# A hybrid decoder layer on one core: mix-out product by halves of its features, square and token sums at later places, and two seven-product feature pairs in each gate-value product with half of their weight sums added by DMA

## The chip, the core and the metric

The kernel runs on one core of a Trainium2 chip. The metric is the device time of one execution in microseconds (us), smaller is better. Before the change three runs gave 2009.51, 2010.1 and 2012.91 us, a median of 2010.1 us.

The engines are named as in the profile: PE (TensorE, matmuls; PEld is its weight load), DVE (VectorE), ACT (ScalarE), POOL (GpSimd) and SP (SyncE, which issues nearly all transfers). A queue name with a q (SPq) is the engine's sequencer.

## What is computed

One decoder layer for 256 tokens of width 2048, all in float32, with a batch of one and depth one:

```python
h = x
hn = rmsnorm(h, norm_mix_w)
q, k, v, g_ret, xr, yr, g_a, g_b = split(hn @ w_in)          # 2048 x 14336
ret = head_groupnorm(chunkwise_retention(rotary(q), rotary(k), v), ret_gn_w)
ret_out = silu(g_ret) * ret
hr = rg_lru(causal_dwconv(xr, rnn_conv_w, rnn_conv_b), ...)  # gated linear recurrence
rnn_out = gelu(yr) * hr
merged = sigmoid(g_a) * (ret_out @ w_proj_ret) + sigmoid(g_b) * (rnn_out @ w_proj_rnn)
h = h + merged @ w_mix_out
h = h + memory_cross_attention(rmsnorm(h, norm_xa_w), rmsnorm(mem, norm_mem_w), ...)
up = causal_dwconv(rmsnorm(h, norm_ffn_w) @ ffn_w_up, ...)   # 2048 x 11264: gate | value
gate, val = split(up)
h = h + (silu(gate) * val) @ ffn_w_down                      # 5632 x 2048
return rmsnorm(h, final_norm_w)
```

## The kernel before

**Precision.** Each float32 operand is split into a high part (a cast to fp32r) and a low part (the rest), and a product is three matmuls: high by high, low by high, high by low. Weights are split in `weight_parts` (lines 338 to 345): ACT casts `hi` (L343), DVE subtracts to get `lo` (L344). The parts stand in six buffers each, `PART_BUFS`.

**Weight stream.** All weights lie in one array in HBM, in the order in which they are used. `prefetch` (L267) takes them in chunks of 1 MB through SP's queue into one of three `raw` buffers, two chunks ahead of the product that uses them. A chunk of a plain product (`steps_n`) holds four feature tiles of 128 rows by 512 columns; a chunk of a paired product (`steps_pair`, L469) holds two feature tiles (a k-pair) of two column blocks. Such a chunk costs PE 24 matmuls of 128 x 512.

**Seven products.** In a paired product, a k-pair, two halves of the tokens and two column blocks make a product of 2 x 2 blocks by 2 x 2 blocks. For the k-pairs named in a tuple such as `SEVEN = (2, 5)` it is done with seven block products in place of eight, so 21 matmuls in place of 24. This needs sums of tokens (`sums_of`, L436: four DVE operations, one more on DVE and one on ACT for the split, and one DVE addition where only the split parts are at hand) and sums of weights (`seven_parts`, L358): from the blocks b12, b11, b22, b21 of the chunk DVE makes four sums in place (L364), b11+b12, b12+b22, b11+b12+b22 and b11+b12+b22+b21, each 128 x 512. A chunk in seven products has three and a half `hi`/`lo` pairs of 128 x 1024 to make, a plain one two. `token_sums` (L434) keeps every sum by its tile, so that a second product with the same tokens finds it. The queries, values and gates are made by paired and plain products, the eleven gate-value products of the FFN (`up`, L1229) by paired ones with `SEVEN_U = (4,)`.

**Buffers.** Most activations come out of one pool of 29 slots of 4 KB per partition, called `big`; smaller ones out of a pool of ten, `tmp`. A slot is free again when the last reader of its tile is done. PSUM has three double banks (`acc`) and two single banks (`small`); a paired product takes all three and both.

**Work beside the products.** `later(n, fn)` (L371) puts work n+1 chunks behind the current one. `by_dma` (L538) turns a [tokens, features] block into [features, tokens]: ACT writes 16-bit planes (`pl`, L546), two transposing DMAs on SP's queue write `pt`, and one or more chunks later `join` has ACT put the words together again (`f`, L559) and hands them on, to `turn_merged` (L969) for the merged gates.

**Order around the mix-out product.** The last product ahead of it is the second pair of `w_proj_ret` (L987), which gives the merged features of blocks 2 and 3. They reach PE through `by_dma` and `turn_merged`, block 2 joined behind one chunk (wait 1), block 3 behind three (wait 3). `residual` (L997) multiplies with `w_mix_out`, four column blocks of four chunks each. With `in_turn` (L125) the stream holds the first three chunks of blocks 0 and 1, then the last of each, then blocks 2 and 3. At the same place SP loads the residual rows (`hrow`, L993) and the memory rows (`mnat`, L994), and `memory_steps` (L1034) has ACT sum the squares of the memory rows (`sum_squares`, L632) in the first four chunks of the product.

**Recurrence.** In the loop at L911, `recur` (L877) makes for each feature tile two small matmul groups into a `small` bank, which ACT reads at once (`tr`, L889, and `ti`, L890; `ti` is a `big` tile).

Of the kernel before, what the change touches and what calls it, by code (L numbers as in the profile page):

```python
# [14 lines left out]
ALU = mybir.AluOpType  # L15
AX = mybir.AxisListType

P = 128
# [22 lines left out]
EARLY = [2, 2, 4, 4, 4]  # L41
SEVEN = (2, 5)
SEVEN_O = (3, 5)
SEVEN_U = (4,)

O_Q, O_K, O_V, O_G = 0, 1024, 2048, 4096
O_XR, O_YR, O_GA, O_GB = 6144, 8192, 10240, 12288
# [18 lines left out]
    return c  # L66


def both(w, c, seven=SEVEN, row=0, nk=NT, apart=BW):

    return w, row, nk, (c, c + apart, seven)


def weight_plan():

    plan = []
    for g in range(2):
        keys = [("w_in", 0, NT, c + g * BW) for c in (O_Q, O_K)]
        values = [("w_in", 0, NT, O_V + b * BW) for b in range(2)]
        plan += keys + [both("w_in", O_V + 1024)] if g else [keys[0], values[0], keys[1], values[1]]  # L80
        plan.append(both("w_in", O_G + g * 1024))
    for b in range(4):
        plan += [("w_in", 0, NT, c + b * BW) for c in (O_XR, O_YR)]
    plan += [("w_in", 0, NT, O_GB + b * BW) for b in range(2)] + [both("w_proj_rnn", 0)]
    plan += [both("w_in", O_GB + 1024), both("w_proj_rnn", 1024)]
    plan += [both(w, c + b * BW) for w, c in (("w_in", O_GA), ("w_proj_ret", 0)) for b in (0, 2)]
    plan += [("w_mix_out", 0, NT, b * BW) for b in range(4)]
    plan += [(w, 0, NT, b * BW) for b in range(4) for w in ("xa_w_k", "xa_w_q")]
    plan += [("xa_w_v", 0, NT, b * BW) for b in range(4)]
    plan += [both("xa_w_o", 0, SEVEN_O)] + [("xa_w_o", 0, NT, b * BW) for b in (2, 3)]  # L90
    for kind, *a in ff_plan():
        if kind == "down" and sum(a) < NF // 4:
            plan += [both("ffn_w_down", b * BW, SEVEN, a[0] * BW, 4 * a[1]) for b in (0, 2)]
        elif kind == "down":
            plan += [("ffn_w_down", a[0] * BW, 4 * a[1], b * BW) for b in range(4)]
        else:
            plan.append(both("ffn_w_up", a[0] * BW, SEVEN_U, apart=FF))
    return plan


# [26 lines left out]
    return [c for o in products for c in o[:-1]] + [o[-1] for o in products]  # L127


def weight_stream():  # L130

    out = [
        [(w, row + k * P, n, (*c[:2], k // KH in c[2]) if isinstance(c, tuple) else c) for k, n in pieces(i, nk, c)]
        for i, (w, row, nk, c) in enumerate(weight_plan())
    ]
    out[:2] = [[one for pair in zip(*out[:2]) for one in pair]]
    out[-4:-1] = [in_turn(out[-4:-1])]
    i = [c[0][0] for c in out].index("w_mix_out")
    out[i : i + 2] = [in_turn(out[i : i + 2])]
    return [one for chunks in out for one in chunks]  # L140


def chunk(inputs, name, row, n, c):

    if isinstance(c, tuple):
        a, b = (chunk(inputs, name, row, n, one) for one in c[:2])
        order = (b[:, 0], a[:, 0], b[:, 1], a[:, 1]) if c[2] else (a[:, 0], a[:, 1], b[:, 0], b[:, 1])
        return np.stack(order, axis=1)
# [11 lines left out]
def hybrid_layer(  # L160
# [106 lines left out]
    def prefetch(n):  # L267
        while len(ahead) < n and taken[0] < len(stream):
            i = taken[0]
            name, row, nk, c = stream[i]  # L270
            taken[0] += 1
            if i == 0:
                both = wp.tile([P, KC, BW], F32, tag="raw", bufs=RAW_BUFS, name=nm("raw"))
                flat = both.rearrange("p k n -> p (k n)")[:, 0 : NT + KH * (S + BW)]
                cut = NT + S + BW
                for cs in (slice(0, cut), slice(cut, NT + KH * (S + BW))):
                    load(flat[:, cs], head[:, cs], True)
                both = flat[:, NT:].rearrange("p (k n) -> p k n", k=KH)
                scale0.append(flat[:, 0:NT])
                landed.append(flat[:, 0:1])  # L280
                raw = both[:, :, S:]
                xs.raw.append(both[:, :, 0:S])
            else:
                if isinstance(c, tuple):
                    nk *= 2
                size = nk * P * BW
                src = wall[at[0] : at[0] + size].rearrange("(p k n) -> p k n", p=P, k=nk)
                at[0] += size
            if i == 0:
                pass  # L290
            elif i < 4:
                raw = big([P, KH, BW], s="raw")
                if i == 1:
                    landed.append(raw[:, 0, 0:1])
                elif i == 2:
                    behind_of(raw, landed[0])
                    tc.keep_in_program_order(pool.tensor_copy(pa[:, 0:NT], scale0[0]))
            else:
                raw = wp.tile([P, KC, BW], F32, tag="raw", bufs=RAW_BUFS, name=nm("raw"))
            k2 = row // (KH * P)  # L300
            early = i < 2 * len(EARLY)
            own = early and i % 2 == 0
            cuts = () if i == 0 else range(0, nk + 1, KH) if i < 6 else (0, nk)
            if own:
                xs.load(k2 + 1)
            for a, b in zip(cuts, cuts[1:]):
                with tc.issue_after(behind[-1]) if i in in_order else nullcontext():
                    load(raw[:, a:b, :], src[:, a:b, :], early)
                if own and a == 0:
                    xs.load(k2 + nk // KH)  # L310
            if i >= 6:
                load_x(min(4, 2 * i - 11))
            if i == 8:
                load(cid, consts[:, 0:C_DEC], True)
                load(pa[:, 16:P], by_feature[:, 16:P], True)
                load(pb, by_feature[:, P : P + 80], True)
            if i == 13:
                load(pf.rearrange("p a n -> p (a n)"), by_feature[:, P + 80 :], True)
            if i in (8, 9):
                for b in (2 * i - 16, 2 * i - 15):  # L320
                    sum_squares(xin[b], ss0, b)
            if isinstance(c, tuple) and c[2]:
                ahead.append(((row, c), seven_parts(raw)))
                continue
            parts = []
            for k in range(0, nk, KH):
# [31 lines left out]
    def seven_parts(raw):  # L358
# [7 lines left out]
        q2, q4 = weight_parts(raw[:, 2:4])  # L366
        return [p1, p3, p2, q1, q3, q2, q4]

    pending, step = [], [0]

    def later(n, fn):  # L371
# [3 lines left out]
    def chunks(nk, w, row, c):  # L375
# [4 lines left out]
        for k, n in pieces(i, nk, c):  # L380
            prefetch(1)
            (r_, c_), parts = ahead.pop(0)
            assert (r_, c_) == (row + k * P, (*c[:2], k // KH in c[2]) if isinstance(c, tuple) else c)
            prefetch(AHEAD)
            yield k, n, parts
            step[0] += 1
# [79 lines left out]
            sums_of(t, src, scale)  # L466
        out.append(t)

    def steps_pair(w, row, st, nk, c1, c2, seven=SEVEN):  # L469

        last = max(seven)
        banks, begun = {}, set()
# [8 lines left out]
                begun.add(name)  # L481

        o1 = o2 = None
        for k0, n, parts in chunks(nk, w, row, (c1, c2, seven)):
# [322 lines left out]
    for g in range(2):  # L807
# [16 lines left out]
                v = gemm_n("w_in", 0, xs, NT, O_V + b * BW) if b else ended(v_steps)  # L824
                vs.append(split_rows(v, rs0))
        if g == 1:
            vs += [split_rows(v, rs0) for v in pair("w_in", 0, xs, NT, O_V + 1024, O_V + 1024 + BW)]
        qr, kr = turned
        gates = []
        c = O_G + g * 1024  # L830
        for a in pair("w_in", 0, xs, NT, c, c + BW):
# [3 lines left out]
            dve.scalar_tensor_tensor(out=a, in0=t, scalar=1.0, in1=a, op0=ALU.add, op1=ALU.mult)  # L835
            gates.append(a)
        retain(g, qr, kr, vs, dec, gates)


    lam = pb[:, 0:16]  # L840
# [70 lines left out]
    for b in range(4):  # L911
# [28 lines left out]
        def gelu_y(f, xr=xr):  # L940
# [29 lines left out]
        for pr in range(2):  # L970
            merged.append(split_pair(f[:, 2 * pr : 2 * pr + 2, :], 0.5))

    ts = [tanh_rows(big([P, 2, BW], s="sig"), gemm_n("w_in", 0, xs, NT, O_GB + b * BW)) for b in range(2)]
    mb = []
# [22 lines left out]
    def residual(w, st, out, wcol, steps=None):  # L997
# [231 lines left out]
    def up(b, hid, seven):  # L1229
# [4 lines left out]
            conv(f, NF + 4 * b, vl)  # L1234
            gate_up(gt, vl, hid, seven)

        two = pair("ffn_w_up", 0, h2s, NT, b * BW, FF + b * BW, SEVEN_U)
# [62 lines left out]
```

## Time and profile before

| What | Value |
|---|---|
| Median of 3 runs | 2010.1 us (2009.51 to 2012.91) |
| Profiled execution, its own time | 2011.37 us |
| Its span in the profile | 2009.4 us |
| PE busy | 1971.7 us (98%), 8831 matmuls |
| DVE busy | 1564.5 us (78%) |
| ACT busy | 1370.1 us (68%) |
| POOL busy | 25.4 us (1%) |
| Read from HBM | 388.39 MB, 194 GB/s over the span |

The page gives busy time by engine, the span in forty slices, the chain of work that ended last, and the costliest groups of instructions. A group's line reads: source line, engine, operation, what it writes and reads, shape, count, then busy time, mean ns of one, and the idle time ahead of them with its releaser. A row of the view of waits reads: who waited, for whom, us in total, times, longest. A row of the timeline reads: start, length, engine, line, operation, tiles, count, and in brackets the idle time before it with its releaser. A row of the view of windows gives for each stretch its length, the busy time of each engine, the granted PE clock, the share of the DMA engines' time and GB/s. A row of transfers gives the count, the size of one and the median time from issue to landing.

### The profile page before, as it was taken

To read this page: it belongs to the slowest core of one execution; us is meant where nothing else is said; L and a number is where in the kernel's file an instruction comes from. 1 tells how busy PE (TensorE), PEld (TensorE's weight loads), DVE (VectorE), ACT (ScalarE), POOL (GpSimd) and SP (SyncE) were. 2 spreads that over 40 slices of the span, in tenths; PEclk is the share of its full clock that TensorE was granted. 3 is DMA by queue.
4 is the path that set the end of the run, shared out by engine and by line. 5 is a ranking of instruction groups with operands and counts; after the bars stand their busy time and mean duration, and the time that the engine had idled before them with its cause. 6 is when DMAs were issued, how large, how long until landed. Compare 5 with 4: busy or idle time off the path is not lost.

```text
span 2009.4 us, 24019 instructions
## 1 busy us (share of the span) xinstructions
PE 1971.7 (98%) x8831; PEld 1635.7 (81%) x8831; DVE 1564.5 (78%) x2044; ACT 1370.1 (68%) x1671; POOL 25.4 (1%) x25
## 2 busy tenths in 40 slices
PE   9999999998999999699999999999999999999998
PEld 8888788887888888588888888888888888888887
DVE  6887987898788888557546568678889868899686
ACT  6666658987645656568666666877877477874683
POOL 0000001000000000000000000000000000000000
PEclk9999999999999999899999999999999999999999
DMA  8756566666465465868666665756666656666673
GB/s 329 234 212 176 207 223 199 199 202 206 169 229 189 170 228 189 272 209 255 216 199 210 198 194 200 235 199 212 208 223 212 235 189 218 204 223 223 221 238 119
DMA packets 197190, 425.62 MB, mean 212 GB/s; under 512 B 142032, under 2 KB 146640, under 8 KB 152016
## 3 DMA queue, kind: packets, MB, share of 16 engines
q1 hardware_dynamic: 197072, 424.09, 63.2%
q8 instruction: 69, 1.13, 0.2%
q14 instruction: 49, 0.40, 0.1%
HBM read 388.39 MB, written 2.10 MB: 194 GB/s over the span
## 4 chain that ended last, share of the span: by engine, by line
PE 92%; DVE 3%; ACT 2%; issue 1%; DMA 1%; SPq 0%; POOL 0%; POOLq 0%; DVEq 0%; ACTq 0%
PE acc L245 67%; PE sm L245 25%; DVE lo L344 1%; ACT hi L343 1%; ACT f L559 0%; DMA nat<-in_mem 0%; ACT pl L546 0%; DVE tb L728 0%; DVE xr L925 0%; PE warm L242 0%; DVE rows L572 0%; DMA pt<-pl 0%; DVE ta L732 0%; DVE raw L364 0%; DVE fv L1127 0%
## 5 line engine op out<-in xcount | busy, mean ns | idle before, releaser
L245 PE MATMUL acc<-hi,s 128*128 128x512 f32 (+1 forms) x3974 | 1221.9, 389 | 17.2 <-ACT s L582 17.1
L344 DVE TENSOR_TENSOR lo<-raw,hi 128x1024 fp32r<-128x1024 f32 (+1 forms) x796 | 933.4, 1197 | 337.2 <-ACT hi L343 328.4
L343 ACT CAST hi<-raw 128x1024 fp32r<-128x1024 f32 (+1 forms) x796 | 792.4, 1023 | 419.0 <-PE acc L245 145.5
L245 PEld LDWEIGHTS acc<-hi,s 128*128 128x128 f32 x3974 | 745.5, 188 | 170.5 <-ACT s L582 17.6
L245 PE MATMUL acc<-lo,s 128*128 128x512 f32 (+1 forms) x1987 | 772.1, 389 | 1.7 <-DVE lo L344 1.7
L245 PEld LDWEIGHTS acc<-lo,s 128*128 128x128 f32 x1987 | 374.1, 188 | 79.4 <-DVE lo L344 2.5
L245 PE MATMUL sm<-hi,s 128*128 128x512 f32 x1336 | 411.3, 389 | 0.0
L245 PEld LDWEIGHTS sm<-hi,s 128*128 128x128 f32 x1336 | 250.8, 188 | 52.0
L245 PE MATMUL sm<-lo,s 128*128 128x512 f32 x668 | 260.0, 389 | 0.0
L559 ACT COPY f<-pt 128x1024 uint16<-128x1024 uint16 x128 | 167.0, 1353 | 35.5 <-DMA pt<-pl 33.9
L245 PEld LDWEIGHTS sm<-lo,s 128*128 128x128 f32 x668 | 125.4, 188 | 26.0
L364 DVE TENSOR_TENSOR raw<-raw 128x512 f32<-128x512 f32 x164 | 113.1, 690 | 2.5
L245 PE MATMUL acc<-hi,ts 128*128 128x512 f32 x246 | 76.8, 394 | 1.4 <-ACT hi L343 1.4
L546 ACT COPY pl<-rows 128x1024 uint16<-128x1024 uint16 x56 | 55.7, 1042 | 21.6 <-DVE rows L570 12.2
L546 ACT COPY pl<-o 128x1024 uint16<-128x1024 uint16 x52 | 51.6, 1039 | 6.4 <-DVE o L989 6.4
L245 PEld LDWEIGHTS acc<-hi,ts 128*128 128x128 f32 x246 | 46.3, 189 | 11.7 <-ACT hi L343 2.2
L245 PE MATMUL acc<-lo,ts 128*128 128x512 f32 x123 | 49.0, 398 | 1.1 <-DVE lo L344 1.1
L1127 DVE SCALAR_TENSOR_TENSOR fv<-f,pf,fv 128x255 f32<-128x255 f32 (+1 forms) x88 | 38.6, 482 | 0.0
L524 DVE TENSOR_TENSOR o<-o,acc 128x512 f32<-128x512 f32 x52 | 33.4, 687 | 6.1 <-PE acc L245 6.1
L1127 DVE SCALAR_TENSOR_TENSOR fg<-f,pf,fg 128x255 f32<-128x255 f32 (+1 forms) x88 | 35.8, 479 | 0.0
L514 DVE TENSOR_TENSOR o<-o,acc 128x512 f32<-128x512 f32 x52 | 35.6, 685 | 0.0
L524 DVE TENSOR_TENSOR o<-o,sm 128x512 f32<-128x512 f32 x52 | 34.4, 688 | 0.3 <-PE sm L245 0.2
(193 smaller groups left out, 1011.1 us busy)
## 6 DMA issues: line engine op xcount, KB each, us to landing
raw<-in_wall SPq DMA_DIRECT2D x352, 1024.0 KB, 4.8
nat<-in_x SPq DMA_DIRECT2D x8, 512.0 KB, 9.2
raw<-in_wall SPq DMA_DIRECT2D x7, 512.0 KB, 5.9
pt<-pl SPq DMA_TRANSPOSE x128, 3.3
nat<-in_mem SPq DMA_DIRECT2D x4, 512.0 KB, 8.8
xt<-in_x_t SPq DMA_DIRECT2D x3, 512.0 KB, 8.9
xt<-in_mem_t SPq DMA_DIRECT2D x3, 512.0 KB, 5.5
dec<-in_consts SPq DMA_DIRECT2D x2, 512.0 KB, 4.4
```

What stands on the lines that cost most here:

```text
L245: tc.keep_in_program_order(pe.matmul(*a, **k))
L343: act.copy(hi[:, cs], src[:, cs])
L344: dve.tensor_tensor(out=lo[:, cs], in0=src[:, cs], in1=hi[:, cs].bitcast(F32), op=ALU.subtract)
L364: dve.tensor_tensor(out=o, in0=a, in1=b, op=ALU.add)
L514: dve.tensor_tensor(out=o, in0=a, in1=b, op=op)
L524: dve.tensor_tensor(out=o, in0=o, in1=banks[a], op=ALU.add)
L546: act.copy(planes[:, tt], words[:, tt])
L559: act.copy(halves_[:, :, :, cs], turned_[:, :, :, cs])
L1127: dve.scalar_tensor_tensor(out=y[:, s:S], in0=z[:, j, 0 : S - s], scalar=pf[:, 2 - s, t : t + 1], in1=y[:, s:S], op0=ALU.mult, op1=ALU.add,)
```

## The change

It has six parts. Line numbers here are those of the kernel before.

1. *Gate-value products.* `SEVEN_U` becomes (2, 5), two k-pairs in seven products in place of one, in each of the eleven. Their chunks are stored as b11, b22, b21, b12, and `prefetch` no longer brings them with one load: SP loads b12 twice into the first two quarters of the buffer (a source read twice), POOL issues a DMA that adds b11 and b22 to them in place, SP loads b11 into a `tmp` tile and b22, b21 into the other two quarters. DVE then makes two sums in place of four.
2. *Value pair of the second head group.* `SEVEN_V = (5,)`: one k-pair in seven products in place of two.
3. *Token sums of the input.* `token_sums` is emptied after the retention loop, so that the sums of the input tokens are made anew for the third gate product.
4. *Token sums of the recurrent output.* They are made behind chunks of the first `g_b` product, from the split parts, and no longer with the recurrence.
5. *Mix-out product.* `by_halves`: the stream and the loop take the first two chunks of blocks 0, 1 and 2, then the last two of each, then block 3.
6. *Square sums of the memory rows* move from chunks 0 to 4 of that product to chunks 5 to 9; the last merged block is joined two chunks behind its transposes in place of three.

```diff
-SEVEN_U = (4,)
+SEVEN_U = (2, 5)
+SEVEN_V = (5,)
...
-        plan += keys + [both("w_in", O_V + 1024)] if g else [keys[0], values[0], keys[1], values[1]]
+        plan += keys + [both("w_in", O_V + 1024, SEVEN_V)] if g else [keys[0], values[0], keys[1], values[1]]
...
-            plan.append(both("ffn_w_up", a[0] * BW, SEVEN_U, apart=FF))
+            plan.append(both("ffn_w_up", a[0] * BW, SEVEN_U, apart=FF, added=True))
...
+def by_halves(products):
+
+    return [c for part in (slice(0, 2), slice(2, 4)) for o in products for c in o[part]]
...
-    out[i : i + 2] = [in_turn(out[i : i + 2])]
+    out[i : i + 3] = [by_halves(out[i : i + 3])]
...
+            if isinstance(c, tuple) and c[2] == 2:
+                b11 = tmp("b11").rearrange("p a n -> p (a n)")
+                load(raw[:, 0:2], src[:, 3:4, :].to_broadcast([P, KH, BW]), False)
+                pool.dma_start(out=raw[:, 0:2], in_=src[:, 0:2, :], accum_op=ALU.add)
+                load(b11, src[:, 0, :], False)
+                load(raw[:, 2:4], src[:, 1:3, :], False)
+                ahead.append(((row, c), seven_added(raw, b11)))
+                continue
...
+    def seven_added(raw, b11):
+
+        (p1,) = weight_parts(b11[:, None, :])
+        p3, p2 = weight_parts(raw[:, 2:4])
+        q1, q3 = weight_parts(raw[:, 0:2])
+        for i in (2, 3):
+            b = 0 if i == 2 else 2
+            dve.tensor_tensor(out=raw[:, i], in0=raw[:, b], in1=raw[:, i], op=ALU.add)
+        q2, q4 = weight_parts(raw[:, 2:4])
+        return [p1, p3, p2, q1, q3, q2, q4]
...
         retain(g, qr, kr, vs, dec, gates)
+    token_sums.clear()
...
-                with_sums(rnn, SEVEN, o, 0.5)
+                rnn.append(split_pair(o, 0.5))
...
+    for b in range(2):
+        ts.append(tanh_rows(big([P, 2, BW], s="sig"), gemm_n("w_in", 0, xs, NT, O_GB + b * BW)))
+        if b == 0:
+            for i, k2 in enumerate(SEVEN):
+                later(1 + 2 * i, lambda k2=k2: sums_of(rnn[k2]))
...
-            by_dma(m, turn_merged, 1 + 2 * (b + i == 3))
+            by_dma(m, turn_merged, 1 + (b + i == 3))
...
-                    for one in products[:2]:
-                        for _ in range(NT // KC - 1):
+                    for one in products[:3]:
+                        for _ in range(2):
                             next(one)
...
-                later(c, lambda c=c: sum_squares(mnat[c], ss, c))
-            later(4, lambda: rsms.append(rstd_rows(ss)))
+                later(5 + c, lambda c=c: sum_squares(mnat[c], ss, c))
+            later(9, lambda: rsms.append(rstd_rows(ss)))
```

More of the change, by code (lines that the diff above doesn't have):

```diff
@@ L66, in constants, with both @@
     return c
-def both(w, c, seven=SEVEN, row=0, nk=NT, apart=BW):
-    return w, row, nk, (c, c + apart, seven)
+def both(w, c, seven=SEVEN, row=0, nk=NT, apart=BW, added=False):
+    return w, row, nk, (c, c + apart, seven, added)
 def weight_plan():
@@ L127, in in_turn @@
     return [c for o in products for c in o[:-1]] + [o[-1] for o in products]
+def by_halves(products):
+    return [c for part in (slice(0, 2), slice(2, 4)) for o in products for c in o[part]]
 def weight_stream():
     out = [
-        [(w, row + k * P, n, (*c[:2], k // KH in c[2]) if isinstance(c, tuple) else c) for k, n in pieces(i, nk, c)]
+        [(w, row + k * P, n, (*c[:2], (k // KH in c[2]) * (1 + c[3])) if isinstance(c, tuple) else c) for k, n in pieces(i, nk, c)]
         for i, (w, row, nk, c) in enumerate(weight_plan())
@@ L146, in chunk @@
         a, b = (chunk(inputs, name, row, n, one) for one in c[:2])
-        order = (b[:, 0], a[:, 0], b[:, 1], a[:, 1]) if c[2] else (a[:, 0], a[:, 1], b[:, 0], b[:, 1])
-        return np.stack(order, axis=1)
+        orders = (
+            (a[:, 0], a[:, 1], b[:, 0], b[:, 1]),
+            (b[:, 0], a[:, 0], b[:, 1], a[:, 1]),
+            (a[:, 0], b[:, 1], a[:, 1], b[:, 0]),
+        )
+        return np.stack(orders[c[2]], axis=1)
     w = np.asarray(inputs[name])[0][row : row + n * P, c : c + BW].reshape(n, P, BW)
@@ L382, in chunks @@
             (r_, c_), parts = ahead.pop(0)
-            assert (r_, c_) == (row + k * P, (*c[:2], k // KH in c[2]) if isinstance(c, tuple) else c)
+            assert (r_, c_) == (row + k * P, (*c[:2], (k // KH in c[2]) * (1 + c[3])) if isinstance(c, tuple) else c)
             prefetch(AHEAD)
@@ L467, in with_sums, with steps_pair @@
         out.append(t)
-    def steps_pair(w, row, st, nk, c1, c2, seven=SEVEN):
+    def steps_pair(w, row, st, nk, c1, c2, seven=SEVEN, added=False):
         last = max(seven)
@@ L483, in steps_pair @@
         o1 = o2 = None
-        for k0, n, parts in chunks(nk, w, row, (c1, c2, seven)):
+        for k0, n, parts in chunks(nk, w, row, (c1, c2, seven, added)):
             k2 = k0 // KH
@@ L826, in hybrid_layer @@
         if g == 1:
-            vs += [split_rows(v, rs0) for v in pair("w_in", 0, xs, NT, O_V + 1024, O_V + 1024 + BW)]
+            vs += [split_rows(v, rs0) for v in pair("w_in", 0, xs, NT, O_V + 1024, O_V + 1024 + BW, SEVEN_V)]
         qr, kr = turned
@@ L971, in turn_merged @@
             merged.append(split_pair(f[:, 2 * pr : 2 * pr + 2, :], 0.5))
-    ts = [tanh_rows(big([P, 2, BW], s="sig"), gemm_n("w_in", 0, xs, NT, O_GB + b * BW)) for b in range(2)]
-    mb = []
+    ts, mb = [], []
+    for b in range(2):
[3 more added lines that the diff above has]
+                later(1 + 2 * i, lambda k2=k2: sums_of(rnn[k2]))
     for b in (0, 2):
@@ L1235, in value @@
             gate_up(gt, vl, hid, seven)
-        two = pair("ffn_w_up", 0, h2s, NT, b * BW, FF + b * BW, SEVEN_U)
+        two = pair("ffn_w_up", 0, h2s, NT, b * BW, FF + b * BW, SEVEN_U, True)
         for a, then, wait in zip(two, (lambda f: conv(f, 4 * b, gt), value), (1, 3)):
```

## Prediction, made before the changed kernel ran

> **What bounds the kernel now.** First the page: PE is busy for nearly the whole span, and the two dips in its slices mark two places where it waits.
>
> ```profile
> span 2009.4 us, 24019 instructions
> PE 1971.7 (98%) x8831; PEld 1635.7 (81%) x8831; DVE 1564.5 (78%) x2044; ACT 1370.1 (68%) x1671; POOL 25.4 (1%) x25
> ...
> PE   9999999998999999699999999999999999999998
> ```
>
> PE sets the time. A change gains by giving PE fewer matmuls or shorter waits, and loses by making PE wait. So I read next the view of waits for PE, whole kernel:
>
> ```profile
> PE acc L245 <- ACT s L582: 17.1, 1, 17.1
> PE sm L245 <- ACT ti L890: 8.1, 2, 6.6
> PE acc L245 <- DVE lo L344: 2.8, 4, 1.0
> PE acc L245 <- ACT hi L343: 1.4, 1, 1.4
> ```
>
> Two stalls make 23.7 of some 29 us. The timeline shows the first, at the start of the mix-out product:
>
> ```profile
> 817.44 0.62 PE L245 MATMUL acc<-hi,s 128*128 128x512 f32 x2
> ...
> 835.78 1.69 SPq L216 DMA_DIRECT2D raw<-in_wall  x2
> 841.36 1.06 ACT L634 ACTIVATE nat<-nat 128x1024 f32<-128x1024 f32 x1 [11.97 <-DMA nat<-in_mem]
> ...
> 842.41 2.50 ACT L559 COPY f<-pt 128x1024 uint16<-128x1024 uint16 x2
> ...
> 845.62 1.52 PE L245 MATMUL acc<-hi,s 128*128 128x512 f32 x2 [17.14 <-ACT s L582]
> ```
>
> PE has two chunks of work that need only merged blocks 0 and 1 (817.4 to 828.5, where the idle time of the last row begins). Block 2 is joined by ACT (L559), but ahead of that on ACT stands the square sum of the memory rows, which waits 12 us for its transfer. The windows add what the stall costs behind its end:
>
> ```profile
> 840.00:845.00 5.00, 0.00 (x0) 0.00 (x0) 0.00 (x0) 3.61 (x5) 0.00 (x0) 0.50 1.04 423
> 845.00:850.00 5.00, 4.38 (x10) 3.17 (x11) 1.29 (x2) 4.97 (x7) 0.00 (x0) 0.50 0.83 346
> ...
> 490.00:495.00 5.00, 2.87 (x13) 2.87 (x14) 1.04 (x2) 0.96 (x3) 0.00 (x0) 0.50 0.99 305
> ```
>
> The granted clock (third column from the end) is 0.50 until 850: ten matmuls in 4.38 us. The second stall is in the recurrence, shown by PE's timeline, the chain and ACT's timeline:
>
> ```profile
> 478.48 1.60 PE L245 MATMUL sm<-rp,rp 128*128 128x256 f32 x12
> ...
> 492.13 2.93 PE L245 MATMUL sm<-rp,rp 128*128 128x256 f32 x12 [6.58 <-ACT ti L890]
> ```
>
> ```profile
> 488.32 3.18 DMA pt<-pl
> ```
>
> ```profile
> 491.60 0.84 ACT L890 ACTIVATE ti<-sm,h 128x256 f32<-128x256 f32 x2 [2.71 <-DMA pt<-pl]
> ```
>
> ACT must write `ti` to empty PE's small bank, and waits for a transposing DMA that has nothing to do with it: what it needs is the `big` slot of that DMA's planes. The pool is full here.
>
> **The change, part by part.** *Matmuls.* One k-pair more in seven products saves 3 matmuls in each of eleven gate-value products, the value pair gives 3 back: 30 fewer. One lasts 0.227 us:
>
> ```profile
> 345.50 38.11 PE acc L245 x168
> ```
>
> 30 x 0.227 = **-6.8 us**.
>
> *Mix-out and square sums.* PE now has six chunks before it needs block 2: 817.4 + 6 x 5.44 = 850.1, when the joins are long done, as the built order has them ahead of the square sums. The stall goes: 17.1, and the slow clock with it (ten matmuls in 4.4 us in place of 2.3): 2.1. Next late is the seventh chunk's weight load: it is issued at 835.78, and behind the first memory load (landed 841.36) stand three of 0.52 MB and its own 1.05 MB at 423 GB/s, so 847.6; cast and subtraction (1.04 and 1.22) end at 849.9. That is on time by 0.2 us, so I take a loss of 0.7 (from 0 to 2.4, the next load's time). **-18.5 us**. The earlier join of block 3 hides in the same 32 us.
>
> *Token sums, in the recurrence.* Emptying the sums frees two `big` slots and the later rnn sums two more, so `ti` need not wait: 6.6 us, and 1.3 for the clock (2.93 against 1.60). The 1.5 us of the other wait I leave. **-7.9 us**. The sums made anew are five of some 2.4 us on DVE and 0.6 on ACT, between 500 and 820 us, where DVE is busy for 212 of 250 us and PE without a wait:
>
> ```profile
> 570.00:820.00 250.00, 250.00 (x1105) 207.05 (x1104) 212.49 (x250) 146.97 (x168) 0.00 (x0) 1.00 0.57 205
> ```
>
> They cost nothing there; without that cover they would cost their 12 us.
>
> *Value pair.* Its first seven-product chunk makes PE wait 1.4 and 1.1 us on `hi` and `lo` (the last two rows of waits, in part). With one seven-product chunk less I take back 1.7 of it (from 0 to 2.5). **-1.7 us**. Sum so far: -34.9 us.
>
> *Gate-value products.* This is the doubtful part. The FFN's windows, one product and the whole:
>
> ```profile
> 1338.30:1381.10 42.80, 42.80 (x191) 35.44 (x190) 37.21 (x52) 34.60 (x43) 0.00 (x0) 1.00 0.64 214
> 1295.40:1936.50 641.10, 639.40 (x2817) 528.12 (x2816) 548.00 (x729) 458.80 (x552) 0.70 (x1) 1.00 0.64 213
> ```
>
> DVE, and the first matmuls that use what they make, in the seven-product chunk of that product:
>
> ```profile
> 1347.22 1.23 DVE L344 TENSOR_TENSOR lo<-raw,hi 128x1024 fp32r<-128x1024 f32 x1 [1.77 <-ACT hi L343]
> ...
> 1351.52 0.69 DVE L344 TENSOR_TENSOR lo<-raw,hi 128x512 fp32r<-128x512 f32 x1
> ...
> 1355.32 0.69 DVE L364 TENSOR_TENSOR raw<-raw 128x512 f32<-128x512 f32 x1
> 1355.92 1.22 DVE L344 TENSOR_TENSOR lo<-raw,hi 128x1024 fp32r<-128x1024 f32 x1
> ```
>
> ```profile
> 1358.12 0.62 PE L245 MATMUL acc<-hi,s 128*128 128x512 f32 x2
> ...
> 1360.16 0.61 PE L245 MATMUL acc<-hi,ts 128*128 128x512 f32 x2
> ```
>
> The four weight sums stay four per product (2 x 2), so DVE gets 1.22 + 0.69 = 1.9 us more per product: 39.1 in 42.1 (186 matmuls). It is not the bound on average. But the lead matters: the first `lo` of that chunk is ready at 1348.45, 9.7 us ahead of its matmul, the third at 1357.15, only 3.0 us ahead. One such chunk uses up 6.7 us of lead, of which two sums (1.4) go away: 5.3. Two use 10.6 per product. Before, 6.7 came back over seven plain chunks with 5.6 us of idle DVE; I reckon some 9 can come back over six. Of the missing 1.6 I take half, from 0 to 1.6: 11 x 0.8 = **+9 us**.
>
> The DMA chain comes on top. These rows bound it:
>
> ```profile
> raw<-in_wall SPq DMA_DIRECT2D x352, 1024.0 KB, 4.8
> nat<-in_x SPq DMA_DIRECT2D x8, 512.0 KB, 9.2
> ...
> dec<-in_consts SPq DMA_DIRECT2D x2, 512.0 KB, 4.4
> rgw<-in_rg_w_a SPq DMA_DIRECT2D x4, 256.0 KB, 3.4
> ```
>
> And the waits in the FFN, ACT's for its loads:
>
> ```profile
> ACT hi L343 <- DMA raw<-in_wall: 53.8, 28, 3.7
> ```
>
> Now one load of 4.8 us; then the doubled b12 (256 KB read, 512 KB written: 3.9, between 3.4 and 4.4), and only when it has landed POOL's adding DMA of 512 KB, x us. No row shows an adding DMA, or one of POOL's. x lies between 4.4, a plain load of that size, and 9.2, the same size under load; I take 4.4, as the FFN's DMA engines are at 0.64. The sums are then 3.9 + x - 4.8 = 3.5 us later. In the FFN ACT already waits for 28 loads of some 120, so nothing hides this but the lead. I charge each product what its second such chunk has beyond the 3.0 us of lead: 11 x 0.5 = **+5.5 us**. SP's two extra issues and the b11 load hold nobody up, since its `tmp` slot is free by then; POOL has nothing else queued in the FFN but one small power.
>
> Sum: -34.9 + 14.5 = -20.4. From the profiled execution's own 2011.4: 1991.0; that run lies 1.3 us above the median of 2010.1, so **1990 us**.
>
> A rule of the Trainium skill speaks against my x. Collectives: The Full Stack, in the section on side-by-side accounting ("Why ReduceScatter is half of AllGather"), says an add inside a DMA needs two source reads, so that it moves at half the rate. No row here shows it. What it would do here is the third rival below.
>
> **The rivals.** *The adding DMA is hidden.* Fewer sums per chunk leave the lead where it is, and no gate-value product stalls: 0 to 4 us in place of 14.5, so 1975 to 1980. For it: DVE has 3 us to spare per product and the loads run two chunks ahead. Against it: 28 waits of ACT for loads.
>
> *The adding DMA becomes the bound (slower).* Each product waits x - 0.9 - 3.0 us at its second such chunk. It gives back all of the 34.9 us at 9 + 11(x - 3.9) = 34.9, x = 6.3 us. At the upper bound of 9.2 the time is 2010 - 35 + 67 = 2042; at 7.3, 2021. For it: two transfers stand in a row, on a queue that the traces do not show. Against it: x = 4.4 is what an unhurried 512 KB takes.
>
> *It reads twice*, the sum's old value as well as the weights: another 512 KB at 423 GB/s, 1.2 us. x = 5.6: 9 + 11 x 1.7 = 28, so 2003 us.
>
> *A part doesn't do what it says.* If another tile takes the freed slots, the recurrence's 7.9 us stay: 1998.
>
> **How the numbers follow.** Forecast (1984 to 1997) 0.40; hidden 0.22; reads twice or a part without effect (1997 to 2006) 0.14; about the same as before 0.05; slower 0.19. A measurement of this kernel can tell 0.2%, 4 us, from no change: faster 0.76, same 0.05, slower 0.19. Cases of both signs hold much of the chance: 1984 to 1997 is the forecast's own range. For 8 in 10 the range goes from 1975, all stalls hidden, up to 2021, x = 7.3.
>
> **What would show it.** PE's waits should have lost the rows for `s` L582 and `ti` L890, and slices 10 and 17 of PE be full; a new wait at 850 would be the seventh chunk's load. PE's matmuls should fall by 30. In the FFN, rows for PE waiting on `lo` or `hi` should come to about 15 us, most at the second seven-product chunk; near none means hidden, over 35 the slower rival. The landing time of POOL's transfers decides: 4.4, 5.6 or over 6.3 us. Waits for token sums between 500 and 820, or a stall left at 485, would prove those parts wrong.

## The result, and the profile after

The changed kernel takes 2043.2 us (2039.95 to 2047.7, 4 runs) beside 2011.5 us before on the same chip: a ratio of 1.0159, 95% interval 1.0135 to 1.0183. It is slower by 32 us, where 20 us faster was forecast. The profiled execution, the fastest of the four, spans 2038.1 us, 28.7 more than the one before. Its page first:

```profile
span 2038.1 us, 24178 instructions
PE 1985.0 (97%) x8801; PEld 1632.1 (80%) x8801; DVE 1588.8 (78%) x2077; ACT 1384.3 (68%) x1694; POOL 46.5 (2%) x47
...
PE   9999999999999999999999999998999988999998
```

PE has 30 matmuls fewer, as the change says, and yet is busy for 13 us more. The two dips of before, slices 10 and 17, are full. The new dips lie in the last third, in the FFN. The windows at the three places where something was to be gained, in the changed kernel:

```profile
205.00:230.00 25.00, 24.25 (x106) 19.45 (x105) 24.07 (x46) 17.97 (x20) 0.00 (x0) 1.00 0.54 201
470.00:510.00 40.00, 40.00 (x189) 33.59 (x188) 34.35 (x45) 35.22 (x49) 0.00 (x0) 1.00 0.61 205
800.00:870.00 70.00, 69.91 (x309) 57.57 (x308) 45.90 (x49) 51.07 (x62) 0.70 (x1) 1.00 0.91 294
```

The same windows before:

```profile
205.00:230.00 25.00, 23.05 (x94) 18.14 (x93) 24.20 (x36) 16.89 (x19) 0.00 (x0) 0.93 0.56 212
470.00:510.00 40.00, 33.42 (x153) 28.01 (x152) 28.92 (x39) 31.61 (x45) 0.00 (x0) 0.91 0.46 154
800.00:870.00 70.00, 52.86 (x223) 42.99 (x222) 40.67 (x45) 39.35 (x45) 0.70 (x1) 0.88 0.72 239
```

The second field is PE's busy time with its matmuls. In the same time PE now does 12, 36 and 86 matmuls more: at 0.227 us each 2.7, 8.2 and 19.5 us, 30 us together. GpSimd's small powers mark the stages well, since each follows a norm. The last one ahead of the FFN, and the first at the head behind it, before:

```profile
1299.40 0.70 POOL L651 TENSOR_TENSOR ro<-rv,mhalf 128x2 f32<-128x2 f32 x1 [368.65 <-DVE rv L649]
1995.59 0.55 POOL L1202 TENSOR_TENSOR last<-pt,half 128x1 f32<-128x1 f32 x1 [695.50 <-DVE pt L1201]
```

and in the changed kernel:

```profile
1268.10 0.73 POOL L680 TENSOR_TENSOR ro<-rv,mhalf 128x2 f32<-128x2 f32 x1 [9.54 <-DVE rv L678]
...
2023.87 0.57 POOL L1236 TENSOR_TENSOR last<-pt,half 128x1 f32<-128x1 f32 x1 [89.51 <-DVE pt L1235]
```

The FFN begins 31.3 us earlier. But the stretch between the two marks, 696.2 us before, lasts 755.8: 59.6 us more, with 33 matmuls (7.5 us) less to do by the edit (the windows count 30 fewer). So everything that was gained is lost there, and nearly the same again. PE's waits in the changed kernel, and the window of that stretch:

```profile
PE acc L255 <- DVE lo L362: 26.0, 25, 2.9
PE acc L255 <- ACT hi L361: 12.7, 10, 3.1
```

```profile
1268.10:2023.87 755.77, 714.46 (x3038) 574.98 (x3037) 614.76 (x809) 513.44 (x623) 19.02 (x22) 0.98 0.70 216
```

No single wait is long, the longest is 3.1 us. There are 35 of them. By PE's timeline some 8 us of them lie in the first seven-product chunks, 12 in the second ones, and 19 in the plain chunk right behind a second one. What they wait for, from the issues of transfers in the changed kernel (count, size, median from issue to landing):

```profile
raw<-in_wall SPq DMA_DIRECT2D x51, 512.0 KB, 4.9
raw<-in_wall POOLq DMA_DIRECT2D x22, 512.0 KB, 7.0
```

and one such chunk in the chain of work, in order of time (start, length, what):

```profile
1427.25 4.07 DMA raw<-in_wall
...
1431.45 0.60 issue
1432.05 0.01 POOLq L316
1432.07 7.00 DMA raw<-in_wall
...
1439.45 1.06 ACT hi L361
1440.51 0.03 issue
1440.53 1.22 DVE lo L362
1441.76 0.60 DVE raw L394
```

The doubled b12 takes 4.07 us, 0.75 us go by until GpSimd issues, the adding DMA takes 7.00: the sum stands 11.8 us after the first issue. A plain load of twice the size took 4.8. Only then can ScalarE cast it, and VectorE make the other sum. The casts behind it come later too, and PE waits for them, in this product mostly in the chunk behind the second sums:

```profile
1445.81 0.50 PE L255 MATMUL acc<-lo,ts 128*128 128x512 f32 x1 [0.42 <-DVE lo L362]
...
1449.94 0.50 PE L255 MATMUL acc<-lo,s 128*128 128x512 f32 x1 [2.47 <-DVE lo L362]
```

### The profile page after: what moved, and what is told of

The parts are those of the page before. It is cut to its first block, busy times and chain, and to the rows that moved or that the text cites. A ratio compares the mean times of both kernels' runs of the same rounds, so it can differ in the third digit from the quotient of the medians.

```text
span 2038.1 us, 24178 instructions
## 1 busy us (share of the span) xinstructions
PE 1985.0 (97%) x8801; PEld 1632.1 (80%) x8801; DVE 1588.8 (78%) x2077; ACT 1384.3 (68%) x1694; POOL 46.5 (2%) x47
## 3 DMA queue, kind: packets, MB, share of 16 engines
q0 software_dynamic: 3168, 11.54, 3.2%
HBM read 405.69 MB, written 2.10 MB: 200 GB/s over the span
## 4 chain that ended last, share of the span: by engine, by line
PE 69%; DVE 11%; DMA 9%; ACT 8%; issue 3%; SPq 0%; POOL 0%; ACTq 0%; POOLq 0%; DVEq 0%
PE acc L255 53%; PE sm L255 15%; DMA raw<-in_wall 7%; DVE lo L362 4%; ACT hi L361 3%; DMA pt<-pl 2%; ACT f L588 2%; ACT pl L575 1%; DVE fv L1161 1%; ACT o L1275 1%; DVE o L543 1%; DVE fg L1161 1%; DVE raw L394 1%; DVE fo L1171 0%; DVE fo L1172 0%
## 5 line engine op out<-in xcount | busy, mean ns | idle before, releaser
L255 PE MATMUL sm<-hi,s 128*128 128x512 f32 x1256 | 387.5, 390 | 2.4 <-DVE o L553 2.4
L255 PEld LDWEIGHTS sm<-hi,s 128*128 128x128 f32 x1256 | 236.2, 188 | 52.8 <-ACT v L623 2.1
L255 PE MATMUL sm<-lo,s 128*128 128x512 f32 x628 | 244.6, 389 | 0.6 <-DVE lo L362 0.6
L255 PEld LDWEIGHTS sm<-lo,s 128*128 128x128 f32 x628 | 117.9, 188 | 25.9 <-DVE lo L362 1.4
L255 PE MATMUL acc<-hi,ts 128*128 128x512 f32 x306 | 96.7, 397 | 12.7 <-ACT hi L361 12.7
L255 PEld LDWEIGHTS acc<-hi,ts 128*128 128x128 f32 x306 | 56.9, 189 | 28.5 <-ACT hi L361 17.7
L255 PE MATMUL acc<-lo,ts 128*128 128x512 f32 x153 | 62.4, 408 | 7.8 <-DVE lo L362 7.4
L255 PEld LDWEIGHTS acc<-lo,ts 128*128 128x128 f32 x153 | 28.9, 189 | 22.2 <-DVE lo L362 16.9
L316 POOL DMA_DIRECT2D raw<-in_wall x22 | 19.4, 880 | 1002.5 <-DVE lo L362 550.9
L1275 ACT ACTIVATE o<-o,ro 128x512 f32<-128x512 f32 x44 | 29.8, 717 | 14.3 <-DVE o L553 14.3
```

The source lines that it names most:

```text
L255: tc.keep_in_program_order(pe.matmul(*a, **k))
L316: pool.dma_start(out=raw[:, 0:2], in_=src[:, 0:2, :], accum_op=ALU.add)
L1275: act.mul(a[:, tt, :], a[:, tt, :], rs2[:, tt : tt + 1])
```

## The experiments

Each time is a median, with the ratio to the kernel before, run on the same chip, and its 95% interval. "FFN" is the stretch between the two marks of GpSimd.

| Kernel | us | ratio (interval) | FFN, us |
|---|---|---|---|
| before | 2011.5 | | 696.2 |
| changed | 2043.2 | 1.0159 (1.0135 to 1.0183) | 755.8 |
| one seven-product chunk, VectorE adds (u4_plain) | 1982.4 | 0.986 (0.9844 to 0.9877) | 696.7 |
| one, adding DMA (u4_added) | 1979.5 | 0.9841 (0.9827 to 0.9856) | 693.2 |
| one, at the fourth k-pair, adding DMA (u3_added) | 1978.1 | 0.9835 (0.982 to 0.9849) | 693.2 |
| two, VectorE adds (u25_dve) | 1992.2 | 0.9903 (0.9888 to 0.9918) | 707.4 |
| two, no b12 in two sums, one load (no_addition) | 1987.7 | 0.9881 (0.9866 to 0.9896) | 704.1 |
| the same load from GpSimd (pool_alone) | 1985.7 | 0.9867 (0.9852 to 0.9882) | 701.7 |
| two loads in a row, not added (pool_plain) | 2019.2 | 1.0035 (1.0021 to 1.0048) | 735.0 |
| two, adding DMA in the first (add_at_2) | 2009.2 | 0.9994 (0.9983 to 1.0005) | 724.5 |
| two, adding DMA in the second (add_at_5) | 2029.5 | 1.0087 (1.0071 to 1.0103) | 746.2 |
| changed, transfers exchanged (swap) | 2061.7 | 1.0251 (1.0221 to 1.028) | 780.1 |
| changed, asked for earlier (ahead3) | 2066.1 | 1.0272 (1.0255 to 1.0289) | 767.9 |

**Where the loss is.** The gate-value pairs were taken back to one seven-product chunk, first with all sums on VectorE, then with the adding DMA kept.

```diff
-SEVEN_U = (2, 5)
+SEVEN_U = (4,)
-            plan.append(both("ffn_w_up", a[0] * BW, SEVEN_U, apart=FF, added=True))
+            plan.append(both("ffn_w_up", a[0] * BW, SEVEN_U, apart=FF, added=False))
```

> The change with the gate-value pairs as they were: one seven-product chunk each, all four sums on VectorE, no adding DMA. Theory A (all of the loss, and more, sits in the gate-value products): the stages ahead of them end 31 us earlier, as in the changed kernel, and the FFN takes the 696 us that it took before: 2011 - 31 = 1980 us, PE's waits in the FFN about 2 us. Rival B (a part of the loss comes from the other edits, for instance work that they push into the FFN): clearly above 1985.

> One seven-product chunk in each gate-value product, as before, but its b12 sums made by the adding DMA. Theory A1 (what matters is how late the sums come against the lead that PE's stock gives: some 7 us late, against 9.7 us of lead at the first such chunk): few stalls, 1976 to 1986 us, beside 1980 without the addition. Rival A2 (any wait for the addition stops ScalarE's queue and so all casts behind it, whatever the lead): half of the 67 us that the gate-value products lost, so some 2013 us.

With VectorE's sums the FFN is what it was before, 696.7 us, and the rest of the change is worth 29 us. PE's longest waits in that kernel:

```profile
span 1979.3 us, 24013 instructions
...
PE acc L255 <- DVE lo L362: 2.9, 5, 0.8
PE sm L255 <- DVE o L553: 1.5, 2, 1.3
```

With one adding DMA per product, which lands after a median of 6.3 us, nothing is lost, and 3 us are gained (the intervals of the two overlap). So late sums are free while the lead covers them, and A2 falls.

**Two chunks without the addition.** In the first kernel (`added=False`) VectorE makes all four sums of each of the two chunks, from one plain load. In the second the two sums and the layout of the change stay, but one plain load takes the place of the pair of transfers, so that this kernel leaves b12 out of two sums:

```diff
-                load(raw[:, 0:2], src[:, 3:4, :].to_broadcast([P, KH, BW]), False)
-                pool.dma_start(out=raw[:, 0:2], in_=src[:, 0:2, :], accum_op=ALU.add)
+                load(raw[:, 0:2], src[:, 0:2, :], False)
```

> The change with two seven-product chunks in each gate-value product, but all eight sums of a product on VectorE and one plain load per chunk, no adding DMA. Theory A (the two transfers in a row are the loss): 1980 less 7.5 for 33 matmuls, plus stalls for the lead that VectorE's 6.7 us per chunk use up, 5 to 20 us: 1978 to 1993 us. Rival C (two dense chunks in one product exhaust the stock of casts whoever adds): about as the change, 2030 to 2045 us.

> The change with the same two sums per chunk on VectorE and the same casts, but in place of the doubled load and POOL's adding DMA one plain 512 KB load from SyncE: b12 is left out of two of the weight sums, the other work is as in the change. Theory A (the chain of two transfers is the loss): 1980 - 7.5 = 1972, plus 0 to 9 us for the lead: 1972 to 1982 us. Rival C (the layout itself, with its small loads, casts and two such chunks, is the loss): 2030 to 2045 us.

Both are far from the changed kernel's 2043 us, so rival C falls. If the second chunk only saved its 33 matmuls, both would take 1982.4 - 7.5 = 1974.9 us; they take 17.3 and 12.8 us more. That is what the second chunk costs without the pair of transfers, and I read it as the price of the lead. For the second kernel I had expected 0 to 9, too little. The remaining 51 to 55 us come with the pair of transfers.

**What of the pair costs: the queue, the row of two, or the addition.** In the first kernel GpSimd's transfer stays behind the doubled load but writes over it (`accum_op` left out). In the second, whose edit is shown, it stands alone. Both leave b12 out of two sums.

```diff
-                load(raw[:, 0:2], src[:, 3:4, :].to_broadcast([P, KH, BW]), False)
-                pool.dma_start(out=raw[:, 0:2], in_=src[:, 0:2, :], accum_op=ALU.add)
+                pool.dma_start(out=raw[:, 0:2], in_=src[:, 0:2, :])
```

> The change with POOL's DMA writing its 512 KB over the doubled b12 without adding it, behind the same wait: b12 is left out of two weight sums, the queue, the order and the bytes from HBM stay. Theory S (the addition itself is slow, since it reads the sum's old value too): the transfer lands after about 4.9 us, as plain 512 KB do, in place of 7.0, the sums come 2.1 us earlier, and of the 51 us some 11 x 2 x 2.1 = 46 go if every chunk pays for it: 1995 to 2012 us. Rival Q (two transfers in a row, and POOL's queue, are the price, the addition is nearly free): landing stays near 7, time 2035 to 2045 us.

> The change with one plain 512 KB load from POOL's queue in place of the doubled load and the adding DMA: b12 is left out of two weight sums. It differs from the kernel with the plain load from SyncE (1988 us) in the queue alone, and from the one with POOL's unadding transfer behind the doubled load (2019 us) in the wait for that load alone. Theory W (standing behind another transfer is what costs): 1986 to 1996 us. Rival Q (POOL's queue is what costs): 2010 to 2022 us.

The issues of 512 KB, first with the plain load from SyncE, then alone on GpSimd's queue, then behind the doubled load without adding:

```profile
raw<-in_wall SPq DMA_DIRECT2D x44, 512.0 KB, 4.6
```

```profile
raw<-in_wall POOLq DMA_DIRECT2D x22, 512.0 KB, 5.2
```

```profile
q0 software_dynamic: 3168, 11.54, 1.6%
...
raw<-in_wall POOLq DMA_DIRECT2D x22, 512.0 KB, 5.6
```

GpSimd's queue lands 0.6 us later than SyncE's, and that costs nothing: 1985.7 beside 1987.7. The doubled load ahead costs 2019.2 - 1985.7 = 33.5 us: the wait for it and its traffic together, since it also reads 11.5 MB more from HBM (405.69 against 394.16). The runs do not separate the two, but the plain 1 MB loads land after 4.9 us in both kernels, which speaks for the wait. The addition itself costs the other 24: 7.0 in place of 5.6 us. With it goes a change in the changed kernel's row for GpSimd's queue (packets, MB, share of the 16 DMA engines' span):

```profile
q0 software_dynamic: 3168, 11.54, 3.2%
```

The same packets and bytes hold the DMA engines twice as long: 3.2% of 2038.1 us over 22 transfers is 3.0 us each, against 1.6% of 2017.3, 1.5 us. Theory S expected more to go (1995 to 2012), rival Q nothing; the price is shared between them.

**Which of the two chunks pays.** The adding DMA serves one chunk of the product, VectorE makes the sums of the other.

```diff
-        [(w, row + k * P, n, (*c[:2], (k // KH in c[2]) * (1 + c[3])) if isinstance(c, tuple) else c) for k, n in pieces(i, nk, c)]
+        [(w, row + k * P, n, (*c[:2], (k // KH in c[2]) + (k // KH in c[3])) if isinstance(c, tuple) else c) for k, n in pieces(i, nk, c)]
-            plan.append(both("ffn_w_up", a[0] * BW, SEVEN_U, apart=FF, added=True))
+            plan.append(both("ffn_w_up", a[0] * BW, SEVEN_U, apart=FF, added=(2,)))
```

> Two seven-product chunks per gate-value product, the b12 sums by the adding DMA in the first of them alone, all four sums of the second on VectorE. Theory L (a stock of lead per product: the first such chunk hides the late sums, as the single one did at 1979 us, and the second finds the stock used up): near the kernel without any addition, 1988 to 2000 us. Rival E (each adding DMA costs the same beside a second such chunk): half of the 51 us between 1992 and 2043, so some 2017 us.

> The mirror case: VectorE makes all sums of the first seven-product chunk, the adding DMA serves the second alone. Theory L: most of the loss is here, 2010 to 2040 us, and clearly more than with the addition in the first chunk. Rival E: some 2017 us, the same as with the addition in the first chunk.

Against 1992.2 the first adds 17 us, the second 37; together 54, about the 51 of both. Neither theory held as written: adding in the second chunk costs twice as much, as theory L said, but adding in the first, which is free when it stands alone, is not free once another follows. With the addition in the first chunk PE waits some 7 us in the first chunks themselves, so not all of the 17 is passed on to the second.

**Two ways to save it.** The transfers were exchanged, so that the adding DMA reads the doubled b12; and the chunks were asked for three ahead (`AHEAD = 3`).

```diff
-                load(raw[:, 0:2], src[:, 3:4, :].to_broadcast([P, KH, BW]), False)
-                pool.dma_start(out=raw[:, 0:2], in_=src[:, 0:2, :], accum_op=ALU.add)
+                load(raw[:, 0:2], src[:, 0:2, :], False)
+                pool.dma_start(out=raw[:, 0:2], in_=src[:, 3:4, :].to_broadcast([P, KH, BW]), accum_op=ALU.add)
```

> The change with the two transfers exchanged: SyncE loads the 512 KB of b22-side weights plainly, POOL's DMA adds b12, doubled, so that the adding DMA reads 256 KB from HBM in place of 512. Theory S (the adding DMA is slow by its read and write of the 512 KB sum in SBUF, not by what it reads from HBM): landing near 7.0, time 2035 to 2048 us. Rival H (the reads from HBM set it): landing near 6, time 2015 to 2030 us.

> The change with its weight chunks asked for three chunks ahead in the program rather than two, with the same three raw buffers. Theory B (loads wait for a raw buffer to come free, not for their place in the program, so the chain cannot start earlier): 2035 to 2048 us. Rival F (the chain starts a chunk, some 5 us, earlier and most of its lateness is hidden): 1985 to 2015 us.

Both are slower than the change, and outside what either theory of each had said. The exchanged addition, in the rows of its kernel:

```profile
q0 software_dynamic: 5984, 11.54, 3.2%
...
HBM read 405.69 MB, written 2.10 MB: 198 GB/s over the span
...
raw<-in_wall POOLq DMA_DIRECT2D x22, 512.0 KB, 9.6
```

It comes in nearly twice the packets and lands after 9.6 us, which neither theory expected. It was meant to read half as much from HBM, but the changed kernel reads the same 405.69 MB: against the kernel with one plain load (394.16) that is 512 KB more for each doubled b12, so the 256 KB are read twice. Rival H, that reads from HBM set the landing, is therefore not tested by this run. Asking earlier does not help: the adding DMAs then land after 8.9 us. That kernel also loses some 14 us ahead of the FFN (its mark comes at 1282.0 us), so its time is no clean measure of the chain. Of these, 6.0 us are waits of PE for `ti` in the recurrence:

```profile
PE sm L255 <- ACT ti L920: 6.0, 3, 4.1
```

The rest was not divided.

**The other steps,** each undone in the kernel with one seven-product chunk (1982.4 us):

| Undone | us | ratio (interval) |
|---|---|---|
| mix-out by halves, back to turns of two products (in_turn) | 1988.5 | 0.9883 (0.9867 to 0.99) |
| the late square sums (squares_first) | 1988.7 | 0.9885 (0.9869 to 0.99) |
| the emptied token sums (no_clear) | 1985.0 | 0.9866 (0.9851 to 0.9881) |
| the late recurrence sums (sums_at_once) | 1989.2 | 0.9885 (0.9871 to 0.99) |

```diff
-    out[i : i + 3] = [by_halves(out[i : i + 3])]
+    out[i : i + 2] = [in_turn(out[i : i + 2])]
-                    for one in products[:3]:
-                        for _ in range(2):
+                    for one in products[:2]:
+                        for _ in range(NT // KC - 1):
```

> The change with its gate-value pairs as before (1982 us), and the mix-out's first two products chunk about as before, not by halves; squares late and the earlier join stay. Theory M (the cover of six chunks is what removes the stall; two chunks end 10.9 us after the start, and the join of block 2 comes when its planes are turned, some 3 to 6 us later, plus 2 for the clock): 1985 to 1990 us. Rival N (the late squares alone remove it): 1981 to 1984 us. Rival O (the whole stall returns): near 2000 us.

```diff
-                later(5 + c, lambda c=c: sum_squares(mnat[c], ss, c))
-            later(9, lambda: rsms.append(rstd_rows(ss)))
+                later(c, lambda c=c: sum_squares(mnat[c], ss, c))
+            later(4, lambda: rsms.append(rstd_rows(ss)))
```

> The change with its gate-value pairs as before (1982 us), and the square sums of the memory rows back at their early place, the mix-out by halves kept. Theory M (six chunks of cover, 32 us, are enough even when the joins stand behind the squares): the join of block 2 comes no later than the 842 us of before, its product is due at 841 + 0 to 9: 0 to 3 us lost, 1982 to 1985 us. Rival N (it was the place of the squares that made the stall): the wait for the joined block returns in part, 5 to 17 us: 1987 to 1999 us.

```diff
-    token_sums.clear()
```

> The change with its gate-value pairs as before (1982 us), but the token sums stay in their slots, so the recurrence has two big slots fewer. Theory P (either two slots suffice): 1981 to 1984 us and no wait of PE for ti. Rival Q (all four are needed): PE's wait for ti returns, 6.6 us and the slow clock behind it, 1988 to 1992 us.

```diff
-                rnn.append(split_pair(o, 0.5))
+                with_sums(rnn, SEVEN, o, 0.5)
-                later(1 + 2 * i, lambda k2=k2: sums_of(rnn[k2]))
+                pass
```

> The change with its gate-value pairs as before (1982 us), but the sums of the recurrence's output are made at once, as before, so their two big slots are taken while it runs; the token sums are emptied. Theory P (either two slots suffice): 1981 to 1984 us, no wait for ti. Rival Q (all four are needed): 1988 to 1992 us.

The time with turns is in theory M's range (1985 to 1990), that with early squares in rival N's (1987 to 1999), though not by the wait that N names. With turns of two products and the late squares, the join of block 2 comes 4.0 us late, as the waits of that kernel show:

```profile
PE acc L255 <- ACT s L611: 4.0, 1, 4.0
```

With halves and early squares the joined block is no longer waited for. But ScalarE stands 7.1 us before its first square until the memory rows land, as its timeline shows; joins and the second square follow, and the casts behind them come at 839.0, too late for PE by 1.6 us:

```profile
830.20 1.06 ACT L663 ACTIVATE nat<-nat 128x1024 f32<-128x1024 f32 x1 [7.08 <-DMA nat<-in_mem]
...
839.04 1.98 ACT L361 CAST hi<-raw 128x1024 fp32r<-128x1024 f32 x2
```

So either edit removes most of the 17.1 us, and undoing it beside the other costs some 6 us, with intervals that just overlap that of the 1982.4. In the profiled executions 4.9 and 3.4 us of this lie ahead of the FFN (marks at 1273.6 and 1272.2 beside 1268.7); the rest lies in the FFN, which these edits leave as it is, and has no cause shown.

In the recurrence, with the emptying alone undone, the wait for `ti` stays at 0.5 us, and the FFN's mark comes at the same 1268.7 us: the late sums suffice there, and the 3 us that this kernel is slower lie in the FFN, without a cause shown. With the sums made at once PE waits for `ti` three times, 3.2 us in all, and the mark comes 4.5 us later. So emptying alone removes 4.9 of the 8.1 us, not all, and the time, 1989.2, is in rival Q's range; theory P held for one pair of slots and not for the other.

```profile
PE sm L255 <- ACT ti L920: 3.2, 3, 1.8
```

## Why the prediction was wrong

**Right:** the matmuls (30 fewer), the mix-out (18.5 said, 19.5 by the matmuls done in the same time), the recurrence (7.9 and 8.2) and the value pair (1.7 said; 12 matmuls more in its window, less the 3 that came in, make 2.0). The terms ahead of the FFN, with those 3 matmuls, come to 27.4 us, and its mark comes 31.3 earlier; the other 4 were not traced. PE's full slices 10 and 17 and the vanished waits for `s` and `ti` are the signs that were named. The wait for the seventh chunk's load, for which 0.7 us were set aside, did not come. The rest of the change alone, with one chunk per gate-value product, gains 29 us, shown by the first experiment.

**Wrong:** "I take 4.4, as the FFN's DMA engines are at 0.64", the latency of the adding DMA, and with it the term of 5.5 us. The adding DMA landed after 7.0 us (median, 5.8 to 10.3), beyond the 6.3 that had been worked out as the point from which the change loses. So it is the rival with the adding DMA as the bound that came true, held at 0.19. My reason against it, that 4.4 is what an unhurried 512 KB takes, compared it with a transfer that neither adds nor stands behind another nor goes through GpSimd's queue. The runs put a price on each, in time to landing: 0.6 us for the queue, 0.4 for the transfer ahead, 1.4 for the addition, on top of 4.6. The doubled b12, put down as 256 KB read, was read twice from HBM, 512 KB, but its landing in the chunk shown, 4.07 us, is near the 3.9 said. With the 0.75 us until GpSimd issues, which I had left out, the sum is 4.07 + 0.75 + 7.0 - 4.8 = 7.0 us late, not 3.5. By the prediction's own rule, 11 times what goes beyond 3.0, that makes 44 in place of 5.5 us. (The rival's own sum at x = 7.0 gives 2018, still 25 short: it left out the 0.75 us as well, and put the first chunk at nothing.)

Measured were 51 to 55 us for the pair of transfers. The rule, that each product pays once for what its second chunk has beyond the lead, gave 44, somewhat less than that, and not its place: 17 us come with the addition in the first chunk, and half of PE's waits fall in the plain chunk behind the second. It also counted only the wait. Two kinds of loss sit in the window of the FFN: 755.77 - 714.46 = 41.3 us of idle PE, and 714.46 us for matmuls that take 694.57 less 7.5 with one chunk per product, 27.4 us more:

```profile
1268.73:1965.38 696.65, 694.57 (x3068) 573.96 (x3067) 587.22 (x779) 493.91 (x598) 0.70 (x2) 1.00 0.63 210
```

(that row is the kernel with one chunk and VectorE's sums). By an estimate from the granted clock, 0.98 over 755.8 us, the slow clock makes some 15 of the 27; the rest was not divided. I had charged the slow clock to the two stalls that the change takes away, and not to those that it brings.

The lead's own term, 9 us, bounded at 18, measured 12.8 with the change's two sums (17.3 with all four on VectorE): too small, within its bounds.

The rule of the Trainium skill that was named, in Collectives: The Full Stack ("Why ReduceScatter is half of AllGather"), that an add inside a DMA needs two source reads and halves the rate, stands there for the reduce of collectives; GpSimd's queue agrees with it here: 3.0 against 1.5 us of all DMA engines for the same bytes. The rival that used it added 1.2 us, and 1.4 was measured; it failed because it added them to 4.4.

**A version that beats both:** one seven-product chunk per gate-value product with the adding DMA, 1978.1 (at the fourth k-pair) and 1979.5 us, 32 to 33 us below the kernel before. For the fourth k-pair 1972 to 1980 us were expected if the lead covers the late sums; its adding DMAs land after 7.6 us and still cost nothing: the FFN takes 693.2 us with either.

## What to carry to other kernels

A DMA that adds into what another DMA has just written is two latencies in a row, and holds the DMA engines twice as long as a plain one: price it by the chain from first issue to landing, not by a plain transfer of its size. Compare that chain with the lead of the chunk that needs it: with one such chunk per product a chain of some 11 us was free, with two it cost 51 to 55. When a change takes away stalls and brings others, charge the slow clock to both.

## What the runs showed of the hardware

TensorE's granted clock fell behind some short waits. In the changed kernel a wait of 3.12 us was followed by some six microseconds at about half the pace (0.63 against 0.39 us for the single matmul); the rows of the two stretches, with the granted clock as third figure from the end, follow the matmuls. The last two rows are the stretches behind a single wait of 2.86 us and behind one of 2.47 us:

```profile
1425.77 1.22 PE L255 MATMUL acc<-hi,ts 128*128 128x512 f32 x2 [3.12 <-ACT hi L361]
...
1428.72 0.63 PE L255 MATMUL acc<-lo,s 128*128 128x512 f32 x1
...
1432.29 0.39 PE L255 MATMUL acc<-lo,s 128*128 128x512 f32 x1
```

```profile
1427.87:1431.71 3.84, 3.84 (x10) 3.01 (x9) 3.84 (x7) 3.84 (x6) 0.00 (x0) 0.50 0.82 277
1432.29:1436.00 3.71, 3.71 (x18) 3.06 (x17) 3.23 (x4) 2.60 (x3) 0.66 (x1) 1.00 1.03 293
1776.20:1779.00 2.80, 2.79 (x8) 2.18 (x9) 2.80 (x4) 2.58 (x4) 0.00 (x0) 0.59 0.00 0
1449.94:1453.00 3.06, 3.06 (x13) 2.55 (x14) 3.06 (x5) 2.35 (x3) 0.00 (x0) 1.00 0.21 80
```

So a wait of 2.86 us brought the clock down (it was 1.00 from 1770.0 to 1773.3, ahead of it), and one of 2.47 did not.

TensorE: Matmul & The Clock Gate, in the Trainium skill (Part 1, The HAM clock gate), gives some 3.4 us of idleness for this; here 2.86 sufficed.

With a source doubled by a broadcast the adding DMAs came in 5984 packets in place of 3168, for the same bytes, and landed after 9.6 us in place of 7.0; that the packets are the reason was not shown. Doubling by a broadcast saved no reads from HBM: the kernels with either order of the transfers read 405.69 MB, the one with a single plain load in their place 394.16, so each doubled 256 KB was read twice.
